# A decoder block's Out projection: its last block product made of seven inner products, interleaved with the sixth

## The chip, the cores and the metric

The kernel runs on one core of a Trainium2 chip. The metric is the device time of one launch in microseconds (us). A core has TensorE (PE, matrix products into PSUM), VectorE (DVE), ScalarE (ACT), GpSimd (POOL) and SyncE (SP); the last two issue most transfers here. Transfers move between the chip's memory (DRAM) and the on-chip SBUF, or inside SBUF.

## What is computed

One layer of a trunk on 512 tokens of width 2048: a windowed attention, its output projection, then a gate of embeddings and two norms. Cut to what matters:

```python
def swa_mixer(h, w_in, w_out, sinks, rel_bias):
    ...
    return (out * jax.nn.silu(gate)) @ w_out

def reference(x, p, norm_g, final_g, ...):
    hn = rmsnorm(x, norm_g[i])
    y = swa_mixer(hn, ...)
    x = x + y
    emb = p[i] @ ple_proj[i]
    g = jax.nn.sigmoid(rmsnorm(x, ple_norm[i]) @ ple_gate[i])
    x = x + emb * g
    return rmsnorm(x, final_g)
```

`w_out` and `ple_gate` are 2048 x 2048. The change touches the product with `w_out`.

## The kernel before

**Three matmuls for one.** Values are float32, but TensorE runs the faster type fp32r. So each operand is split in a high part (a cast on ScalarE) and a low part (the operand less its high part, on VectorE), and `mm3` (L120 to L126) issues three matmuls: high x high, high x low, low x high.

**Seven products for eight.** Out projection and gate projection cut both matrices in 2 x 2 blocks and make seven block products (numbers 1 to 7) in place of eight, from sums and differences of blocks. `ORDER_OUT` is 1, 7, 2, 6, 5, 3, 4. A block product multiplies 256 tokens by 1024 x 1024 weights. It runs over two column halves `jj`, four pieces of weights `m` in each (128 x 1024, 512 KiB, two chunks of 128 rows by 512 columns), two chunks `kk` and two token blocks `tb`: a piece is 12 matmuls, a block product 96. The last one, product 4, uses the activations' block 22 as it is.

**Weights.** `Pieces` (object `B`) numbers the pieces in the order of their use. `ahead(i)`, called as piece `i` is used, loads pieces up to `i + 3` on SP's queue and splits pieces up to `i + 2`: `bhi` on ScalarE (L641), `blo` on VectorE (L642). Raw, high and low parts have three buffers each (`wpool`). Sums of weight blocks for products 7, 5 and 6 are made in DRAM long before. Product 6's eight pieces are loaded into tiles `grown`; after their use, accumulating transfers on GpSimd's queue (L628) add block 21 of `w_out`, which makes product 4's pieces.

**Activations.** `Forms.steps(p)` makes the activations of product `p`: a subtraction in place (L734), then four times a cast `fh` and a low part `fl` (L746, L747), in eight buffers of `acts`.

**Results.** `add_y` adds each finished PSUM bank into `x1` on VectorE, once or twice (L955, L957), and where a block of `x1` is complete, `squares` sums its squares on ScalarE (L924). The functions waiting to be called stand in `later`; `some_later` issues them spread over the next pieces.

**Turns.** The gate projection needs `x1` transposed. `turn(kp, th, tag)` issues four transposes of 128 x 128 on TensorE into a PSUM bank (L938) and two copies scaled by `pn` on ScalarE (L941). Twelve of the sixteen turns stand in product 4, two after each of six pieces; the last four stand in the gate's first product.

**PSUM.** Four tags with two banks each: `s` and `p` hold product 1's two column halves, in whose banks 6, 5 and 3 go on, then product 4's; `t` and `o` hold those of products 7 and 2, then the turns of product 4.

**Order.** In this stage TensorE and SP run in the order written. VectorE, ScalarE and GpSimd get a fixed order from a planner when the program is built, so work whose buffers are free can stand well ahead of where it is written.

Of the kernel before, what the change touches and what calls it, by code (L numbers as in the profile page):

```python
# [11 lines left out]
F32 = mybir.dt.float32  # L12
# [8 lines left out]
P = 128  # L21
# [34 lines left out]
def trunk_kernel(ctx: ExitStack, tc: tile.TileContext, a: dict):  # L56
# [557 lines left out]
    class Pieces:  # L614
# [3 lines left out]
        def __init__(self):  # L618
            self.specs, self.base, self.made, self.grown, self.due = [], {}, {}, {}, []

# [16 lines left out]
        def _split(self, i):  # L637
            raw = self.base.pop(i)
            hi = wpool.tile([P, WE], F32R, tag="whi", name=f"bhi{i}")
            lo = wpool.tile([P, WE], F32R, tag="wlo", name=f"blo{i}")  # L640
            nc.scalar.copy(hi, raw)  # L641
            nc.vector.tensor_sub(lo, raw, hi.bitcast(F32))  # L642
            self.made[i] = tuple([t[:, :512], t[:, 512:]] for t in (hi, lo))

# [10 lines left out]
        def ahead(self, i):  # L655

            last = len(self.specs) - 9
            for n in range(max(i, 0), min(i + 6, last) + 1):
                kind = self.specs[n][0]
                if n not in self.base and n >= self.done and kind != "grow" and (kind == "seed" or n <= i + 3):  # L660
                    self._prepare(n)
            while self.done <= min(i + 2, last):
                self._split(self.done)
                self.done += 1

        def get(self, i):
            self.ahead(i)

            key = self.specs[i][2]
            if key is not None:  # L670
                n = next((n for n in range(i + 1, len(self.specs)) if self.specs[n][2] == key), None)
                if n is not None:
                    self.due.append((i + 6, n))
            while self.due and self.due[0][0] <= i:
                self._prepare(self.due.pop(0)[1])
            return self.made.pop(i)

    B = Pieces()

    def add_stage(nm, order):  # L680
        at = {}

# [5 lines left out]
        for p in order:  # L688
            for jj in range(2):
                if nm == "ple_gate" and (p, jj) == (4, 0):  # L690
                    for v in range(2):
                        at["e", v] = len(B.specs)
                        add_embeds(p, v)
                at[p, jj] = len(B.specs)
                for m in range(4):
                    if (nm, p) in SUMS:
                        src = summed[nm, p, jj, m]
                    else:
                        src = block(nm, *{1: (1, 1), 2: (2, 1), 3: (2, 2), 6: (1, 1), 4: (2, 1)}[p], jj, m)
                    growing = (6, 4) if (nm, 6) in SUMS else (7, 6, 4)  # L700
# [6 lines left out]
    at_out = add_stage("w_out", ORDER_OUT)  # L707
# [164 lines left out]
    rooms.append(late)  # L872
    x1 = [late.tile([P, NB, 512], F32, name=f"x1_{j}") for j in range(4)]
# [8 lines left out]
    def banks(p, jj, nm):  # L882
# [3 lines left out]
        tag = ("to" if p in (7, 2) else "sp")[jj]  # L886
# [40 lines left out]

    def turn(kp, th, tag):
# [10 lines left out]
        for n in range(2):  # L939
            k = 2 * kp + n  # L940
            nc.scalar.mul(hT[g][:, k % 4, th * 256 : th * 256 + 256], tp[:, n * 256 : n * 256 + 256], pn[:, k : k + 1])  # L941
# [20 lines left out]

    x_at = {(1, 1, 1): 0, (7, 0, 0): 2, (7, 0, 3): 1, (7, 1, 1): 3}
    waiting = {(7, 0): (1, 0), (2, 0): (1, 1)}
    held = {}
    for n, p in enumerate(ORDER_OUT):
        nxt = out_forms.steps(ORDER_OUT[n + 1]) if n < 6 else iter(())
        for jj in range(2):
            later.extend(held.pop(waiting.get((p, jj)), ()))
            calls = iter(range(4))  # L970

            def todo():
                part = x_at.get((p, jj, next(calls)))
                if part is not None:
                    load_x(part)
                next(nxt, None)
                if p == 4:
                    for tag in "to":
                        if turns:
                            turn(*turns.pop(0), tag)  # L980
                    if jj:
                        next(ple_first, None)

            ps = unit(p, jj, at_out, out_forms, todo)
            posts = [partial_of(add_y, p, jj, tb, ps[tb]) for tb in range(2)]
            if p == 1:
                held[p, jj] = posts
            else:
                later.extend(posts)
        run(nxt)  # L990
        if p == 6:
            nc.sync.dma_start(fg, a["final_g"].partition_broadcast(P))
        if p == 3:
            turns = [(kp, 0) for kp in range(8)] + [(kp, 1) for kp in range(4, 8)]
# [78 lines left out]
    spare = late.tile([P, 2 * WE], F32R, name="spare")  # L1073
    rooms4 = {}
    early = {(5, 0, 3): 0, (5, 1, 2): 1, (5, 1, 3): 2, (3, 0, 1): 3, (3, 0, 3): 4, (3, 1, 0): 5, (3, 1, 2): 6}
# [203 lines left out]
```

## Time and profile before

| | us |
|---|---|
| median of three runs | 799.04 (798.94 to 799.8) |
| the profiled execution | 798.73 |
| its span, first to last instruction | 797.0 |
| TensorE busy | 785.5 (99%) |
| VectorE busy | 590.5 (74%) |
| ScalarE busy | 482.7 (61%) |
| GpSimd busy | 149.6 (19%) |

The Out projection's matmuls run from 452.5 to 610.1 us of the span. A row of a group names the line, the engine, the operation and what it writes and reads (`out<-in`), with a count. In a timeline the first number is the start, the second the duration, both in us; the bracket at the end tells how long the engine was idle before and what ended that.

### The profile page before, as it was taken

To read this page: it belongs to the slowest core of one execution; us is meant where nothing else is said; L and a number is where in the kernel's file an instruction comes from. 1 tells how busy PE (TensorE), PEld (TensorE's weight loads), DVE (VectorE), ACT (ScalarE), POOL (GpSimd) and SP (SyncE) were. 2 spreads that over 40 slices of the span, in tenths; PEclk is the share of its full clock that TensorE was granted. 3 is DMA by queue.
4 is the path that set the end of the run, shared out by engine and by line. 5 is a ranking of instruction groups with operands and counts; after the bars stand their busy time and mean duration, and the time that the engine had idled before them with its cause. 6 is when DMAs were issued, how large, how long until landed. Compare 5 with 4: busy or idle time off the path is not lost.

```text
span 797.0 us, 11130 instructions
## 1 busy us (share of the span) xinstructions
PE 785.5 (99%) x3760; PEld 656.1 (82%) x3760; DVE 590.5 (74%) x1013; ACT 482.7 (61%) x992; POOL 149.6 (19%) x363
## 2 busy tenths in 40 slices
PE   9999999999999999999999999999999999999995
PEld 7888888888888888888888888888888888878884
DVE  4436478888877787787887898766656977979686
ACT  5632377677556766566665654555568756758545
POOL 0003013443243314332133200030000020200000
PEclk9999999999999999999999999999999999999998
DMA  8790586889687967879585578998503996885533
GB/s 336 279 212 11 187 237 180 235 211 260 175 226 193 220 199 211 213 207 260 155 220 135 151 267 312 353 258 249 197 26 118 358 208 211 163 212 194 176 106 106
DMA packets 44073, 163.99 MB, mean 206 GB/s; under 512 B 6304, under 2 KB 6944, under 8 KB 40176
## 3 DMA queue, kind: packets, MB, share of 16 engines
q1 hardware_dynamic: 36896, 129.01, 48.1%
q0 software_dynamic: 6832, 33.88, 23.0%
q8 instruction: 29, 0.48, 0.2%
q10 hardware_dynamic: 288, 0.39, 0.1%
q14 instruction: 28, 0.23, 0.1%
HBM read 157.44 MB, written 46.19 MB: 255 GB/s over the span
## 4 chain that ended last, share of the span: by engine, by line
PE 85%; issue 7%; DMA 3%; DVE 3%; POOL 1%; ACT 1%; SPq 0%; DVEq 0%; POOLq 0%; ACTq 0%
PE qps L126 7%; PE qps L124 7%; PE qps L125 7%; PE gps L124 7%; PE gps L125 7%; PE gps L126 7%; PE o L124 6%; PE o L126 6%; PE o L125 6%; PE s L401 2%; PE g L125 2%; PE g L126 2%; PE g L124 2%; PE o L523 2%; PE vps L228 2%
## 5 line engine op out<-in xcount | busy, mean ns | idle before, releaser
L642 DVE TENSOR_TENSOR blo<-braw,bhi 128x1024 fp32r<-128x1024 f32 x80 | 97.7, 1223 | 40.4 <-ACT bhi L641 40.2
L641 ACT CAST bhi<-braw 128x1024 fp32r<-128x1024 f32 x80 | 84.0, 1051 | 56.3 <-PE o L126 16.4
L124 PE MATMUL gps<-xh,whi 128*128 128x512 f32 x256 | 100.5, 393 | 0.0
L125 PE MATMUL gps<-xl,whi 128*128 128x512 f32 x256 | 100.0, 391 | 0.0
L126 PE MATMUL gps<-xh,wlo 128*128 128x512 f32 x256 | 99.9, 390 | 0.0
L503 POOL TENSOR_SCALAR_AFFINE_SELECT own<-r 64x256 fp32r<-64x256 f32 x96 | 61.2, 637 | 193.0 <-ACT r L484 109.3
L113 DVE TENSOR_TENSOR wlo<-wraw,whi 128x1024 fp32r<-128x1024 f32 x60 | 73.5, 1226 | 25.8 <-ACT whi L107 24.3
L124 PE MATMUL qps<-xh,whi 128*128 128x512 f32 x224 | 87.7, 392 | 0.0
L124 PE MATMUL o<-bhi,fho 128*128 128x512 f32 x224 | 87.7, 391 | 0.0
L125 PE MATMUL qps<-xl,whi 128*128 128x512 f32 x224 | 87.4, 390 | 0.0
L126 PE MATMUL qps<-xh,wlo 128*128 128x512 f32 x224 | 87.3, 390 | 0.0
L126 PE MATMUL o<-bhi,flo 128*128 128x512 f32 x224 | 87.2, 389 | 0.0
L125 PE MATMUL o<-blo,fho 128*128 128x512 f32 x224 | 87.2, 389 | 0.0
L461 ACT ACTIVATE t<-t,sm 128x129 f32<-128x129 f32 x128 | 50.6, 397 | 49.3 <-DVE sm L452 46.5
L125 PE MATMUL g<-blo,fhg 128*128 128x512 f32 x192 | 74.8, 390 | 0.4 <-DVE blo L642 0.4
L124 PE MATMUL g<-bhi,fhg 128*128 128x512 f32 x192 | 75.1, 391 | 0.0
L126 PE MATMUL g<-bhi,flg 128*128 128x512 f32 x192 | 74.8, 390 | 0.0
L107 ACT CAST whi<-wraw 128x1024 fp32r<-128x1024 f32 x60 | 62.1, 1037 | 16.1 <-DMA wraw<-in_w_q 16.1
L484 ACT CAST r<-pt 128x256 fp32r<-128x256 f32 x64 | 23.8, 372 | 55.4 <-PE pt L479 55.1
L126 PEld LDWEIGHTS gps<-xh,wlo 128*128 128x128 f32 x256 | 48.1, 188 | 10.6
L124 PEld LDWEIGHTS gps<-xh,whi 128*128 128x128 f32 x256 | 48.1, 188 | 9.1
L125 PEld LDWEIGHTS gps<-xl,whi 128*128 128x128 f32 x256 | 48.1, 188 | 8.7
(204 smaller groups left out, 1699.4 us busy)
## 6 DMA issues: line engine op xcount, KB each, us to landing
wraw<-in_w_gate_in SPq DMA_DIRECT2D x32, 512.0 KB, 5.4
wraw<-in_w_q SPq DMA_DIRECT2D x28, 512.0 KB, 6.2
w_out<-in_w_out POOLq DMA_DIRECT2D x24, 512.0 KB, 7.8
braw<-in_w_out SPq DMA_DIRECT2D x24, 512.0 KB, 4.0
braw<-in_ple_gate SPq DMA_DIRECT2D x24, 512.0 KB, 4.3
w_out<-in_w_out SPq DMA_DIRECT2D x16, 512.0 KB, 7.6
ple_gate<-in_ple_gate SPq DMA_DIRECT2D x16, 512.0 KB, 6.5
ple_gate<-in_ple_gate POOLq DMA_DIRECT2D x16, 512.0 KB, 6.1
```

Source lines behind the costliest of these rows:

```text
L107: nc.scalar.copy(hi, self.raw[i])
L113: nc.vector.tensor_sub(lo, raw, hi.bitcast(F32))
L124: nc.tensor.matmul(ps, sh, mh, start=first, stop=False, skip_group_check=more)
L125: nc.tensor.matmul(ps, sh, ml, start=False, stop=False, skip_group_check=more)
L126: nc.tensor.matmul(ps, sl, mh, start=False, stop=last, skip_group_check=more)
L228: nc.tensor.matmul(v_ps[t], h[:, c], both[:, :, 256:512], start=f, stop=e, skip_group_check=True)
L401: nc.tensor.matmul(s_ps[:, u, : 2 * n], st, key[:, :, first : first + n], start=True, stop=True)
L461: nc.scalar.activation(su, su, AF.Exp, bias=sm[:, u : u + 1], accum_out=sm[:, 2 + u : 3 + u])
L484: nc.scalar.copy(r[:, 0], PT[i])
L503: nc.gpsimd.affine_select(out=cols(own[places[g % 2 ^ low]]), in_=cols(r[here, low].bitcast(F32)), pattern=[[sign * QB, 2], [0, GROUP], [s ...
L641: nc.scalar.copy(hi, raw)
L642: nc.vector.tensor_sub(lo, raw, hi.bitcast(F32))
```

## The change

Product 4 (256 tokens by 1024 x 1024 weights) is cut once more in 2 x 2 blocks, and seven inner products of 128 tokens by 512 x 512 weights are made in place of eight. An inner product has two small steps `n` of 6 matmuls; there are 14. They are written between product 3's eight pieces (`SHARED`): eight of them, then six more at the end.

The weights of the inner products come from the eight grown tiles, four blocks of two tiles each. `Inside.sums` and `Inside.split` add them by transfers from SBUF to SBUF on GpSimd's queue: two copies of block 22 into `sum7`, and eight accumulating transfers. The links run: `sum7` = 22, `sum7` += 12, 12 += 11, and, when the first small product's pieces are split, 11 += `sum7`; after the fourth's, 21 += 11. The inner forms (`Inside.forms`) are made in place in activation block 22, seven of 128 x 512. Their order is 1, 7, 6, 2, 5, 4, 3.

From product 6 to near the end of this stage pieces are loaded four ahead and split three ahead, every fourth into the tile `spare` as a fourth buffer. The growing of a tile is written four pieces after its use and not six. The turns are spread: four in product 3, then one after each of several small steps and two together (kp 6 and 7) after the third of the last six. Those two are copied on VectorE. The load of `final_g` stands after the seventh small step. Product 2 of the gate takes the banks `s` and `p`.

Functions to be called later are now taken half at each step. The core of the diff:

```diff
         def _split(self, i):
-            raw = self.base.pop(i)
-            hi = wpool.tile([P, WE], F32R, tag="whi", name=f"bhi{i}")
-            lo = wpool.tile([P, WE], F32R, tag="wlo", name=f"blo{i}")
+            kind, whose, key = self.specs[i]
+            raw = whose.raw(*key) if kind == "part" else self.base.pop(i)
+            if self.first4 <= i < self.last4 and i % 4 == 3:
+                hi, lo = rooms[1][:, :WE], rooms[1][:, WE:]
+            else:
+                hi = wpool.tile([P, WE], F32R, tag="whi", name=f"bhi{i}")
+                lo = wpool.tile([P, WE], F32R, tag="wlo", name=f"blo{i}")
             nc.scalar.copy(hi, raw)
             nc.vector.tensor_sub(lo, raw, hi.bitcast(F32))
             self.made[i] = tuple([t[:, :512], t[:, 512:]] for t in (hi, lo))
+            if kind == "part":
+                whose.split(*key)
...
-                if n not in self.base and n >= self.done and kind != "grow" and (kind == "seed" or n <= i + 3):
+                if n not in self.base and n >= self.done and kind not in ("grow", "part") and (kind == "seed" or n <= i + (4 if self.first4 <= i < self.last4 - 2 else 3)):
                     self._prepare(n)
-            while self.done <= min(i + 2, last):
+            while self.done <= min(i + (3 if self.first4 <= i < self.last4 - 2 else 2), last):
                 self._split(self.done)
                 self.done += 1
...
-                    self.due.append((i + 6, n))
+                    self.due.append((i + 6, partial_of(self._prepare, n)))
+                elif key[0] == inside.nm:
+                    self.due.append((i + GROW, partial_of(inside.grow, key)))
...
+    GROW = 4
+    FOURTH = 24, 62
+    FINAL_G = 6
+    ORDER_IN = (1, 7, 6, 2, 5, 4, 3)
...
+        def grow(self, key):
+            nm, jj, m = key
+            nc.gpsimd.dma_start(B.grown[key], block(nm, 2, 1, jj, m), accum_op=ALU.add)
+        def begin(self):
+            s7 = rooms[0].tile([P, 2, 2, 512], F32, tag="partial", name="sum7", bufs=2)
+            self.s7 = s7.rearrange("p i k c -> p i (k c)")
+            self.t = {(kh, jj, i): B.grown[self.nm, jj, 2 * kh + i] for kh in range(2) for jj in range(2) for i in range(2)}
+        def sums(self):
+            for i in range(2):
+                nc.gpsimd.dma_start(self.s7[:, i], self.t[1, 1, i])
+                yield
+            for i in range(2):
+                self.grow_by(self.s7[:, i], self.t[0, 1, i])
+                yield
+            for i in range(2):
+                self.grow_by(self.t[0, 1, i], self.t[0, 0, i])
+                yield
+        def grow_by(self, out, more):
+            nc.gpsimd.dma_start(out, more, accum_op=ALU.add)
+        def raw(self, q, i):
+            if q == 7:
+                return self.s7[:, i]
+            return self.t[{1: (0, 0), 6: (0, 0), 5: (0, 1), 2: (1, 0), 4: (1, 0), 3: (1, 1)}[q] + (i,)]
+        def split(self, q, i):
+            if q == 1:
+                self.grow_by(self.t[0, 0, i], self.s7[:, i])
+            elif q == 2:
+                self.grow_by(self.t[1, 0, i], self.t[0, 0, i])
...
+        def forms(self):
+            v = lambda r, c: gates[2 + c][:, :, 256 + r * P : 256 + (r + 1) * P]
+            v11, v12, v21, v22 = v(0, 0), v(0, 1), v(1, 0), v(1, 1)
+            for q in ORDER_IN:
+                src, sub = {
+                    1: (v11, None), 7: (v11, (v21, v11)), 6: (v11, (v22, v11)), 2: (v12, None),
+                    5: (v21, (v21, v22)), 4: (v22, None), 3: (v12, (v12, v11)),
+                }[q]
+                if sub:
+                    nc.vector.tensor_sub(src, *sub)
...
+    SHARED = [(3, 0, 0), (3, 0, 1), "n", (3, 0, 2), "n", "n", (3, 0, 3), "n", (3, 1, 0), "n", "n", (3, 1, 1), "n", "n", (3, 1, 2), (3, 1, 3)]
+    SHARED += ["n"] * (14 - SHARED.count("n"))
+    OUT = [(p, jj, m) for p in (1, 7, 2, 6, 5) for jj in range(2) for m in range(4)] + SHARED
...
+    VECTOR_TURNS = {(6, 0), (7, 0)}
...
+            out, src = hT[g][:, k % 4, th * 256 : th * 256 + 256], tp[:, n * 256 : n * 256 + 256]
+            if (kp, th) in VECTOR_TURNS:
+                nc.vector.tensor_scalar_mul(out, src, pn[:, k : k + 1])
+            else:
+                nc.scalar.mul(out, src, pn[:, k : k + 1])
...
+    def inner_part():
+        x = None
+        for q in ORDER_IN:
+            if q in (1, 7, 2, 4):
+                ps = bank(f"o4_{q}", {1: "t", 4: "t"}.get(q, "o"))
+                x = ps if q == 1 else x
+            else:
+                ps = x
+            for i in range(2):
+                bh, bl = B.get(at)
+                fh, fl = inside.made[q]
+                for kk in range(2):
+                    k = 2 * i + kk
+                    mm3(ps, fh[:, k], fl[:, k], bh[kk], bl[kk], q in (1, 7, 2, 4) and k == 0, k == 3, q in (6, 5, 3))
+                if i == 1:
+                    coming.append(partial_of(add_in, q, ps))
+                yield
+    def add_in(q, ps):
+        whither = {
+            1: [((0, 0), -1)], 2: [((0, 0), 1)], 7: [((1, 1), 1), ((1, 0), -1)], 6: [((1, 0), -1)],
+            5: [((1, 1), 1)], 3: [((0, 1), 1)], 4: [((1, 0), 1)],
+        }[q]
+        for (r, c), sign in whither:
+            j, t = c, 2 + r
+            xt = x1[j][:, t, :]
+            if sign > 0:
+                nc.vector.tensor_add(xt, ps, xt)
+            else:
+                nc.vector.tensor_sub(xt, xt, ps)
+            if q in (2, 5, 3, 4):
+                squares(t, j)
...
+    extra = {
+        (5, 1, 0): [inside.begin, inner_sums, inner_sums], (5, 1, 1): [inner_forms, inner_sums, inner_sums],
+        (5, 1, 2): [inner_forms, inner_sums, inner_sums], (5, 1, 3): [inner_forms], (3, 0, 0): [inner_forms],
+        (3, 0, 1): [partial_of(turn, 0, 0, "o")],
+        (3, 0, 3): [partial_of(turn, 1, 0, "o")],
+        (3, 1, 0): [partial_of(turn, 2, 0, "o")],
+        (3, 1, 1): [inner_forms, partial_of(turn, 3, 0, "o")], (3, 1, 2): [inner_forms], (3, 1, 3): [inner_forms],
+        7: [partial_of(turn, 4, 0, "s")], 8: [partial_of(turn, 5, 0, "s"), ple_first],
+        9: [partial_of(turn, 4, 1, "o"), ple_first], 10: [partial_of(turn, 6, 0, "p"), partial_of(turn, 7, 0, "p")],
+        11: [partial_of(turn, 5, 1, "o"), ple_first],
+        12: [partial_of(turn, 6, 1, "o"), ple_first], 13: [partial_of(turn, 7, 1, "o")],
+    }
...
+    for at, step in enumerate(OUT):
+        if step == "n":
+            next(inner)
+            step, p = seen, None
+            seen += 1
+        else:
+            p, jj, m = step
+            if m == 0:
+                made[p, jj] = part(p, jj)
+                later.extend(held.pop(waiting.get((p, jj)), ()))
+            next(made[p, jj], None)
+        for _ in range(-(-len(later) // 2)):
+            later.pop(0)()
+        later.extend(coming)
+        coming.clear()
+        if step in x_at:
+            load_x(x_at[step])
+        if p in ahead:
+            next(ahead[p], None)
+            if (jj, m) == (1, 3):
+                run(ahead[p])
+        for f in extra.get(step, ()):
+            next(f, None) if hasattr(f, "send") else f()
+        if step == FINAL_G:
...
-                    turn(*turns.pop(0), "s")
+                    turn(*turns.pop(0), "t")
```

More of the change, by code (lines that the diff above doesn't have):

```diff
@@ L705, in add_stage @@
         return at
[L707 removed]
+    add_stage(inside.nm, ORDER_OUT)
     at_ple = add_stage("ple_gate", ORDER_PLE)
@@ L961, in trunk_kernel, with part @@
     turns = []
+    def part(p, jj):
+        ps = banks(p, jj, "o")
+        f = out_forms.made[p]
+        first = p not in (6, 5, 3)
+        for m in range(4):
+            fh, fl = f[m]
+            bh, bl = B.get(at)
+            for kk in range(2):
+                k = 2 * m + kk
+                for tb in range(2):
+                    mm3(ps[tb], fh[:, kk, blk(tb)], fl[:, kk, blk(tb)], bh[kk], bl[kk], first and k == 0, k == 7, not first)
+            if m == 3:
+                posts = [partial_of(add_y, p, jj, tb, ps[tb]) for tb in range(2)]
+                if p == 1:
+                    held[p, jj] = posts
+                else:
+                    coming.extend(posts)
+            yield
@@ L963, in trunk_kernel, with turns_of @@
+    def turns_of(*v):
+        for kp, th, tag in v:
+            turn(kp, th, tag)
     x_at = {(1, 1, 1): 0, (7, 0, 0): 2, (7, 0, 3): 1, (7, 1, 1): 3}
     waiting = {(7, 0): (1, 0), (2, 0): (1, 1)}
[L965 to L991, printed above, removed]
+    held, coming = {}, []
@@ new lines, in trunk_kernel @@
+    inner_sums, inner_forms = inside.sums(), inside.forms()
+    extra = {
[10 more added lines that the diff above has]
+    }
@@ L992, in trunk_kernel @@
             nc.sync.dma_start(fg, a["final_g"].partition_broadcast(P))
-        if p == 3:
-            turns = [(kp, 0) for kp in range(8)] + [(kp, 1) for kp in range(4, 8)]
+    turns = []
     run(ple_first)
```

52 lines of the change are left out of this document (44 added, 8 removed).

## The prediction

> **What bounds the kernel now.** I read the page's first two parts and its chain, then the waits of TensorE, then the stretches around the change.
>
> ```profile
> span 797.0 us, 11130 instructions
> PE 785.5 (99%) x3760; PEld 656.1 (82%) x3760; DVE 590.5 (74%) x1013; ACT 482.7 (61%) x992; POOL 149.6 (19%) x363
> ...
> PE 85%; issue 7%; DMA 3%; DVE 3%; POOL 1%; ACT 1%; SPq 0%; DVEq 0%; POOLq 0%; ACTq 0%
> ```
>
> ```profile
> PE warm_ps L145 <- PEq L1269: 0.8, 1, 0.8
> PE g L125 <- DVE blo L642: 0.4, 1, 0.4
> ```
>
> TensorE is busy for 99% of the span and is most of the chain. Its two longest waits are 0.8 and 0.4 us. So time is gained only by taking matmuls away, and lost only where TensorE starts to wait. The pace inside the Out projection, and the stretches it runs in:
>
> ```profile
> L126 PE MATMUL o<-bhi,flo x224: 389/389/397, 453.0 to 610.1; 128*128 128x512 f32 x112
> ...
> 540.06 0.39 PE L126 MATMUL o<-bhi,flo 128*128 128x512 f32 x1
> ...
> 542.78 0.39 PE L126 MATMUL o<-bhi,flo 128*128 128x512 f32 x1
> ```
>
> ```profile
> 539.70:561.40 21.70, 21.70 (x98) 17.96 (x97) 14.65 (x17) 11.68 (x17) 0.00 (x0) 1.00 0.77 246
> 561.40:583.20 21.80, 21.80 (x98) 18.06 (x97) 13.04 (x15) 11.36 (x17) 0.00 (x0) 1.00 0.50 169
> 583.20:610.30 27.10, 27.10 (x146) 22.93 (x145) 14.73 (x17) 22.03 (x45) 0.00 (x0) 1.00 0.06 20
> 625.00:650.00 25.00, 25.00 (x112) 20.70 (x111) 21.90 (x23) 15.18 (x21) 5.96 (x7) 1.00 1.04 277
> ```
>
> A matmul is shown with 0.39 us because matmuls overlap. What counts is from start to start: between the two rows lie 12 matmuls (one piece of weights: 2 halves x 2 token blocks x 3), 2.72 us, so 0.227 us each. A block product is 96 of them, 21.8 us. The rows of the stretches are length, then busy time of TensorE, weight loads, VectorE, ScalarE and GpSimd, granted clock, DMA share, GB/s. The first three are products 5, 3 and 4. VectorE is busy there for 68%, 60% and 54%, at a full clock (1.00). The fourth lies in the gate projection: VectorE 88%, DMA 104%, and by the waits above TensorE loses nothing there.
>
> **The saving.** Product 4 has 96 matmuls. Seven inner products of 4 weight chunks x 3 have 84, of the same shape (128x128 by 128x512). 12 x 0.227 = **2.72 us** less.
>
> **The transposes.** Twelve turns of four transposes stay, but they stood in six pairs and now stand alone, except one pair.
>
> ```profile
> 586.96 0.40 PE L125 MATMUL o<-blo,fho 128*128 128x512 f32 x1
> ...
> 590.60 0.40 PE L125 MATMUL o<-blo,fho 128*128 128x512 f32 x1
> ...
> 613.67 0.40 PE L125 MATMUL g<-blo,fhg 128*128 128x512 f32 x1
> ...
> 616.88 0.39 PE L125 MATMUL g<-blo,fhg 128*128 128x512 f32 x1
> ```
>
> The first two rows are one piece apart with a pair of turns: 3.64 - 2.72 = 0.92 us a pair (0.89 over the six pieces: 27.1 - 21.76 = 5.34 in all). The last two are one piece and a single turn apart: 3.21 - 2.72 = 0.49. Ten singles and a pair: 4.9 + 0.9 = 5.8 against 5.3, rounded sums of 5.74 and 5.36: **0.4 us** more.
>
> **Splits, forms and sums on VectorE and ScalarE.** Six more splits (14 small steps instead of 8 pieces), three more forms, four subtractions of forms, four more additions into x1. What one costs when another follows at once:
>
> ```profile
> 527.29 1.23 DVE L642 TENSOR_TENSOR blo<-grown,bhi 128x1024 fp32r<-128x1024 f32 x1 [1.45 <-ACT bhi L641]
> 528.44 1.28 DVE L957 TENSOR_TENSOR x<-x,o 128x512 f32<-128x512 f32 x2
> ...
> 539.61 1.28 DVE L957 TENSOR_TENSOR x<-x,o 128x512 f32<-128x512 f32 x2
> 540.80 0.68 DVE L747 TENSOR_TENSOR flo<-gate,fho 128x512 fp32r<-128x512 f32 x1
> 541.40 1.22 DVE L642 TENSOR_TENSOR blo<-braw,bhi 128x1024 fp32r<-128x1024 f32 x1
> ```
>
> ```profile
> 550.69 1.05 ACT L641 CAST bhi<-braw 128x1024 fp32r<-128x1024 f32 x1 [1.29 <-DVE blo L642]
> 551.65 0.62 ACT L924 ACTIVATE junk<-x 128x512 f32<-128x512 f32 x1
> 552.17 0.19 ACT L924 ACTIVATION_READ_ACCUMULATOR junk<-x 128x1 f32 x1
> 552.27 0.62 ACT L924 ACTIVATE junk<-x 128x512 f32<-128x512 f32 x1
> ...
> 553.18 0.62 ACT L746 CAST fho<-gate 128x512 fp32r<-128x512 f32 x1 [0.20 <-PE o L125]
> 553.71 1.05 ACT L641 CAST bhi<-braw 128x1024 fp32r<-128x1024 f32 x1
> ```
>
> ```profile
> 597.88 1.56 ACT L941 ACTIVATE hT<-tp,pn 128x256 f32<-128x256 f32 x4
> 599.31 0.65 ACT L924 ACTIVATE junk<-x 128x512 f32<-128x512 f32 x1
> ...
> L547 DVE TENSOR_TENSOR u<-o,tmp x64: 404/417/430, 118.6 to 456.0; 64x256 f32<-64x256 f32 x64
> ```
>
> From start to start, VectorE: a split 1.15, an addition or a form's low part 0.60. ScalarE: a split's cast 0.96, a square 0.62, a form's cast 0.53, half a turn's copy 1.43/4 = 0.36. Two turns' copies move to VectorE. No row has that operation; bounds are 0.36 (ScalarE's copy) and 0.68 (its 128x512 addition). The nearest row, a 256-wide read of PSUM on VectorE, has 0.42, which I take.
>
> Products 3 and 4 together are now 8 pieces and 14 small steps of 6 matmuls (1.36 us): 21.8 + 19.0 + 5.8 = 46.6 us. VectorE: 22 splits 25.3, 12 additions 7.2, 11 operations of inner forms 6.6, 4 low parts of the gate's first forms 2.4, four copies 1.7, together 43.2, or 93%. ScalarE: 22 x 0.96 + 11 x 0.53 + 8 x 0.62 + 20 x 0.36 = 39.1, 84%. On average both fit, and some inner forms go into product 5's 7 us of free VectorE time.
>
> The crowd is at the end. The last six small steps with seven turns last 6 x 1.36 + 5 x 0.49 + 0.9 = 11.5 us. In them fall, on VectorE, 5 splits 5.8, 4 low parts 2.4, 4 additions 2.4, 4 copies 1.7: 12.3. On ScalarE: 5 casts 4.8, 4 forms 2.1, 4 squares 2.5, 5 turns 3.6: 13.0. The excess is 0.8 and 1.5 us. Against it stands the lead of the splits. With a fourth buffer a split starts three steps ahead: 3 x 1.36 and two turns, 5.05, less cast and subtraction (1.05 + 1.22), is 2.8 us. So by starts nothing reaches TensorE: 0. By full durations (1.05, 0.62, 0.81 with its accumulator read, 0.47) ScalarE has 5.3 + 2.5 + 3.2 + 4.7 = 15.7, 4.2 too much, of which 2.8 is covered: 1.4 us. These are the bounds. The trace runs them back to back at the shorter spacing, so I take a value near the lower one: **0.3 us**. What would be late first is the pair of turns after the third of these steps. It reads x1 after product 3's last two additions, and they can start only when product 3 ends, as the first of these steps begins: 3 x 1.36 + 2 x 0.49 = 5.1 us for two additions of 0.6 with 0.4 of matmul tail, 3.5 us to spare. A late pair holds up every matmul behind it.
>
> **Transfers.** Removed from the way: nothing; the eight accumulating loads that made product 4's weights stay. Added: two copies and eight accumulating transfers from SBUF to SBUF on GpSimd's queue, in a chain: copy of block 22, + block 12, 12 += 11, then (after the first small product's split) 11 += sum. No row shows such a transfer. The nearest are the accumulating loads:
>
> ```profile
> L628 POOL DMA_DIRECT2D grown<-in_w_out x8: 847/856/885, 516.0 to 534.5; - x8
> L628 POOL DMA_DIRECT2D grown<-in_ple_gate x16: 847/855/873, 632.3 to 703.0; - x16
> DMA to landing us min/median/max: 5.1/7.6/11.7
> ...
> grown<-in_w_out POOLq DMA_DIRECT2D x8, 512.0 KB, 10.8
> ...
> fg<-in_final_g SPq DMA_DIRECT2D x1, 1024.0 KB, 16.3
> ```
>
> ```profile
> 520.00:540.00 20.00, 20.00 (x90) 16.57 (x89) 13.02 (x14) 9.98 (x14) 5.14 (x6) 1.00 1.06 239
> 545.02 1.05 ACT L641 CAST bhi<-braw 128x1024 fp32r<-128x1024 f32 x1 [3.86 <-DMA braw<-w_out]
> ```
>
> Issue to landing is 5.1 to 11.7 us; 10.8 is where the engines were full (1.06). The chain runs where the DMA share was 0.77, then 0.50. Ten transfers of 512 KiB at the 239 GB/s of the full stretch are 22 us of all engines. Free in the 540 to 592 us stretch are 5 + 11 + 8 = 24. I take the median, 7.6. The last block to be accumulated was issued at 534.5; the splits that free it now run one piece (2.7) sooner, so it lands at 534.5 - 2.7 + 10.8 = 542.6. Three links later, 565.4, the sums are ready. The last link also waits for the split of the first small product's second half, whose buffer comes free as product 3's first piece ends (561.4 + 2.72 + 2.3 = 566.4). It lands at 574.0. Its reader, the second half of the third small product, comes after five pieces, five small steps and three turns (561.4 + 13.6 + 6.8 + 1.5 = 583.3) and needs its split begun by 581.0. Spare: 7.0 us. Cost: **0**, as long as a link is under (581.0 - 542.6)/4 = 9.6 us.
>
> The ScalarE row is where cover is thinnest: product 5's fourth piece was waited for 3.86 us and was split at 545.02 + 1.05 + 1.22 = 547.3, 0.6 us before TensorE needed it (539.7 + 3 x 2.72 = 547.9). Now the first links fall there. But that load is asked for 2.7 us sooner, and the 1 MB load of final_g (16.3 us in flight, just ahead) moves behind. I cost it at nothing; uncovered, each us later than 2.7 + 0.6 is a us lost. Waiting links block only other links on GpSimd's queue: the next work of that queue, the gate's accumulating loads, starts at 632. SP's order gains one piece of lookahead; final_g and pT stay behind loads not needed for two pieces. Cost 0.
>
> **Sum.** -2.72 + 0.4 + 0.3 = -2.0. The profiled execution took 798.73 us (797.0 and 1.7 around it): 796.7, and a span of 795.0. The median of the three runs is 0.3 above it, so I predict **797.0**.
>
> **Rivals.** A, the links are late. If SBUF to SBUF keeps the 10.8 us of the full stretch, the chain ends at 542.6 + 43.2 = 585.8, 4.8 us after the split's latest start, and TensorE stands before the third small product. 4.8 - 2.3 is 2.5 slower: 801.5. It decides from 9.6 us a link, and turns the sign at 9.6 + 2.3/4 = 10.2. For it: ten more transfers in a chain, and the 11.7. Against: the engines are half free there, and the median is 7.6. Chance 0.13.
> The Trainium skill ("SBUF — State Buffer", section "SBUF: two separate sides") says that a DMA issued from GpSimd can be held up, since VectorE in some modes locks GpSimd out of the port that its descriptors are written through. The trace does not bear that out here: the 16 issues at 847 to 873 ns include those in the stretch with VectorE at 88%, as long as the eight beside an emptier VectorE. By the rule a link would grow by up to one 1.2 us subtraction, 7.6 to 8.8, which takes 1.2 of the 2.0 us that each has to spare and makes A nearer than the rows do.
>
> B, the crowd costs the gain. If VectorE has three splits and three low parts (3 x 1.15 + 3 x 0.6 = 5.3 us) ahead of product 3's last addition, the pair of turns waits 1.8 us beyond the 3.5 to spare: 799.0 - 2.3 + 1.8 = 798.5, no difference to be told. For it: 106% and 113% of work in that stretch. Against: the 88% stretch without a wait. Chance 0.20.
>
> C, a knot of banks. The third early turn takes the PSUM bank of the second small product, whose additions are written out a step later; the later turns alternate in two banks of which each waits for an evacuation. Where a split stands ahead of such an evacuation, TensorE waits for its cast and subtraction, 2.1 us. Three of those: 6.3 - 2.3, 803.0. Against: the pairs of turns before waited for no bank. Chance 0.07.
>
> That the change doesn't make fewer matmuls is excluded by the loops.
>
> **Chances.** About 0.2% (1.6 us) is what a measurement of this kernel can tell from no change. My forecast, 796.4 to 797.4 in its own range (no stall, or 1 us), has 0.60: faster. B 0.20: same. A and C 0.20: slower. The range 796.4 to 801.6 takes in A at 10.8 us a link and leaves out C and A's longer links, 0.12 together, and a little below.
>
> **What would show it.** Right: about 3748 matmuls; products 3 and 4 take 46.6 to 47.3 us; the links land in about 7 to 8 us; no wait of TensorE over 1 us stands between 561 and 612. Wrong: a wait of the third small product's split for a transfer (A), TensorE waiting at the turns for x1 (B), or links over 9.6 us.

## The result, and the profile after

| | before | after |
|---|---|---|
| median, us (lowest to highest) | 799.04 (798.94 to 799.8) | 796.54 (796.14 to 796.99) |
| ratio of the times | | 0.9965 [0.9954, 0.9977] |
| profiled execution, us | 798.73 | 796.17 |
| its span, us | 797.0 | 794.5 |

By the medians of seven executions each the change makes the kernel 2.5 us faster (0.31%), by the ratio 0.35%. The ratio is taken over all executions: their means, 799.26 and 796.48, give it. The page of the changed kernel, its head and its chain; a row of an engine has busy us, share of the span and number of instructions:

```profile
span 794.5 us, 11159 instructions
PE 782.9 (99%) x3748; PEld 653.8 (82%) x3748; DVE 604.7 (76%) x1034; ACT 489.0 (62%) x997; POOL 158.4 (20%) x373
...
PE 83%; issue 9%; DMA 2%; ACT 2%; POOL 2%; DVE 2%; DVEq 0%; POOLq 0%; SPq 0%; ACTq 0%
```

There are 12 matmuls fewer and 21 more operations on VectorE. TensorE is as full as before. Its longest waits:

```profile
PE warm_ps L145 <- PEq L1445: 0.9, 1, 0.9
PE g L125 <- DVE blo L647: 0.6, 1, 0.6
```

Neither stands in the Out projection: the second is the gate's old wait, 0.2 us longer. Where the 2.5 us come from is read from the first and last starts of two groups, the Out projection's first matmul and the gate's first matmul. Before:

```profile
L124 PE MATMUL o<-bhi,fho x224: 387/389/482, 452.5 to 609.6; 128*128 128x512 f32 x112
L124 PE MATMUL g<-bhi,fhg x192: 387/389/477, 610.3 to 756.4; 128*128 128x512 f32 x192
```

After, with the first matmul of product 3 from a timeline:

```profile
L124 PE MATMUL o<-bhi,fho x164: 389/389/476, 452.1 to 592.6; 128*128 128x512 f32 x164
L124 PE MATMUL g<-bhi,fhg x192: 388/389/476, 607.3 to 753.7; 128*128 128x512 f32 x192
...
560.94 0.39 PE L124 MATMUL o<-bhi,fho 128*128 128x512 f32 x1
```

At the trace's finer times the Out projection went from 157.76 to 155.23 us: 2.53 less, all of the gain of the span (2.5). (It starts 0.4 us sooner, and what follows it takes 0.4 longer.) Products 3 and 4 take 607.31 - 560.94 = 46.4 us. Of these 180 matmuls, at 2.72 us for 12, are 40.8, and 5.6 are left for the twelve turns, which took 5.34 before. The stretches around it (length, busy time of TensorE, weight loads, VectorE, ScalarE, GpSimd, granted clock, DMA share, GB/s):

```profile
539.70:561.40 21.70, 21.70 (x98) 17.96 (x97) 13.17 (x16) 10.43 (x15) 4.56 (x6) 1.00 1.03 306
561.40:608.00 46.60, 46.60 (x230) 38.69 (x229) 41.70 (x51) 38.33 (x68) 3.43 (x4) 1.00 0.65 176
596.40:608.00 11.60, 11.60 (x67) 9.74 (x66) 10.22 (x16) 11.59 (x25) 0.00 (x0) 1.00 0.09 13
```

VectorE is at 89% and ScalarE at 82% over the interleaved stretch, and in its last 11.6 us ScalarE is at 100%. TensorE still loses nothing there. The chain of transfers, in GpSimd's timeline (start, duration of the issue, and in brackets what GpSimd waited for), with the medians from issue to landing under it:

```profile
542.19 0.56 POOL L713 DMA_DIRECT2D sum<-grown  x1 [10.20 <-issue]
...
569.42 0.86 POOL L723 DMA_DIRECT2D grown<-sum  x1 [3.96 <-DVE blo L647]
...
sum<-grown POOLq DMA_DIRECT2D x4, 512.0 KB, 6.1
grown<-grown POOLq DMA_DIRECT2D x4, 512.0 KB, 8.1
grown<-sum POOLq DMA_DIRECT2D x2, 512.0 KB, 6.2
```

The first copy starts at 542.19 (forecast 542.6), the last link that product 4's third small product needs is issued at 569.42 and lands 6.0 us later, at 575.4 (forecast 574.0). So far the transfers are what was expected. How near they come to TensorE is seen from ScalarE and TensorE just after:

```profile
576.59 1.05 ACT L646 CAST bhi<-grown 128x1024 fp32r<-128x1024 f32 x1 [1.67 <-PE o L126]
577.55 0.83 ACT L1048 ACTIVATE hT<-tp,pn 128x256 f32<-128x256 f32 x2
...
580.96 0.60 PE L1041 MATMUL tp<-ident,x 128*128 128x128 f32 x4
```

The first row is the cast of the weights that the last link makes; it waited for a buffer that TensorE freed, 1.2 us longer than for the link. Behind it on ScalarE stand the two copies of the second turn. The third turn, at 580.96 on TensorE, goes into the PSUM bank that these copies empty. They end at 578.4, so there are 2.6 us to spare there and 1.2 between landing and cast: some 3.7 us in all.

### The profile page after: what moved, and what is told of

Its sections match the earlier page's. It is cut to its first block, busy times and chain, and to the rows that moved or that the text cites. A ratio compares the mean times of both kernels' runs of the same rounds, so it can differ in the third digit from the quotient of the medians.

```text
span 794.5 us, 11159 instructions
## 1 busy us (share of the span) xinstructions
PE 782.9 (99%) x3748; PEld 653.8 (82%) x3748; DVE 604.7 (76%) x1034; ACT 489.0 (62%) x997; POOL 158.4 (20%) x373
## 4 chain that ended last, share of the span: by engine, by line
PE 83%; issue 9%; DMA 2%; ACT 2%; POOL 2%; DVE 2%; DVEq 0%; POOLq 0%; SPq 0%; ACTq 0%
PE qps L124 7%; PE qps L126 7%; PE qps L125 7%; PE gps L124 7%; PE gps L125 7%; PE gps L126 7%; PE o L126 6%; PE o L124 6%; PE o L125 6%; PE s L401 2%; PE g L125 2%; PE g L126 2%; PE g L124 2%; PE vps L228 2%; PE o L523 2%
## 5 line engine op out<-in xcount | busy, mean ns | idle before, releaser
L647 DVE TENSOR_TENSOR blo<-braw,bhi 128x1024 fp32r<-128x1024 f32 x75 | 91.5, 1223 | 33.1 <-ACT bhi L646 32.8
L646 ACT CAST bhi<-braw 128x1024 fp32r<-128x1024 f32 x75 | 78.9, 1052 | 52.6 <-DMA braw<-in_w_out 11.5
L124 PE MATMUL o<-bhi,fho 128*128 128x512 f32 x164 | 63.9, 390 | 0.0
L126 PE MATMUL o<-bhi,flo 128*128 128x512 f32 x164 | 63.8, 389 | 0.0
L125 PE MATMUL o<-blo,fho 128*128 128x512 f32 x164 | 63.8, 389 | 0.0
```

What stands on the lines that cost most here:

```text
L124: nc.tensor.matmul(ps, sh, mh, start=first, stop=False, skip_group_check=more)
L125: nc.tensor.matmul(ps, sh, ml, start=False, stop=False, skip_group_check=more)
L126: nc.tensor.matmul(ps, sl, mh, start=False, stop=last, skip_group_check=more)
```

## The experiments

All run times below are medians of several runs; each ratio is against the kernel before on the same chip. Several kernels also differ by waits near 494 and 519 us, which come back at the end of this section.

**put_back.** The 12 matmuls are done again: in two of the inner products the first small step is multiplied twice with the same operands, and the accumulation starts over with the second time. Nothing else differs.

```diff
-                for kk in range(2):
+                twice = q in (7, 2) and i == 0
+                for n, kk in enumerate((0, 1, 0, 1) if twice else (0, 1)):
...
-                    mm3(ps, fh[:, k], fl[:, k], bh[kk], bl[kk], q in (1, 7, 2, 4) and k == 0, k == 3, q in (6, 5, 3))
+                    mm3(ps, fh[:, k], fl[:, k], bh[kk], bl[kk], q in (1, 7, 2, 4) and k == 0, k == 3 or (twice and n == 1), q in (6, 5, 3))
```

> The changed kernel with 12 matmuls put back: the first halves of the second and fourth inner products are multiplied twice, the first time into a group that the second one starts anew. Theory M (the time is TensorE's count: 12 x 0.227 = 2.72 us less, about 0.3 us more for turns, all else hidden): 796.5 + 2.7 = 799.2, 0.0% to 0.1% over the kernel before; the span from the Out projection's first matmul to the gate's is 2.7 us longer than in the changed kernel. Rival S (a part of the gain comes from the side edits, buffers, order of loads, later final_g): still faster than before by 0.5 us or more, under 798.5. Rival W (TensorE already waits in the changed kernel, the extra matmuls fill the wait): under 798.0.

Measured: 800.23 us, ratio 1.0007 [0.9997, 1.0016]. The whole gain is gone. In the profiled execution the Out projection takes 159.54 us, 4.3 more than in the changed kernel: 2.72 for the matmuls and 1.6, counted from start to start, around two places where TensorE waits for a low part (TensorE's timeline):

```profile
494.25 0.50 PE L125 MATMUL o<-blo,fho 128*128 128x512 f32 x1 [0.62 <-DVE blo L647]
...
519.39 0.50 PE L125 MATMUL o<-blo,fho 128*128 128x512 f32 x1 [0.30 <-DVE blo L647]
```

Both places are long before the edit.

**less_12.** The kernel before, without the 12 matmuls of the seventh piece of product 4; that part of the result is left out.

```diff
-            for kk in range(2):
+            for kk in range(0 if forms.nm == "o" and (p, jj, m) == (4, 1, 2) else 2):
```

> The kernel before without the 12 matmuls of product 4's seventh piece; its split stays, so one piece of product 4 is left out of the result. Theory M: 2.7 us less than before, 796.3, a ratio of 0.9966, about 0.3 us below the changed kernel since the turns stay in pairs. Rival S: the matmuls alone give less than the changed kernel has, so it stays above 797.0.

Measured: 797.16 us, 0.9966 [0.9954, 0.9977]; the Out projection takes 155.17 us, 2.59 less than before. Twelve matmuls less, with none of the change's other parts, give what the whole change gives. So the count sets the gain, and the parts around it cost TensorE about nothing in sum.

**scalar_turns.** No turn is copied on VectorE.

```diff
-    VECTOR_TURNS = {(6, 0), (7, 0)}
+    VECTOR_TURNS = set()
```

> The changed kernel with the two turns' four copies back on ScalarE: 4 x 0.36 = 1.4 us more there in the last six small steps, where ScalarE is busy for 11.6 of 11.6 us, 1.6 less on VectorE (10.2 of 11.6). Theory L: ScalarE runs late by up to 1.4 us, of which the lead of 1 to 2.8 us covers most: 796.5 to 797.9. Rival B of the prediction (no room left in that stretch): 1.4 us or more lost, over 797.9.

Measured: 796.44 us, 0.9962 [0.9949, 0.9975]; Out projection 155.19 us. Four copies more on ScalarE in its full stretch, four less on VectorE, and nothing moves: the crowd at the end costs nothing on either side of that choice.

**three_buffers.** Splits go back to three buffers and a lead of two steps, loads to a lead of three.

```diff
-    FOURTH = 24, 62
+    FOURTH = 0, 0
```

> The changed kernel without the fourth buffer: loads three ahead and splits two ahead as before. A small step of 1.36 us then leaves a split 2 x 1.36 (less 2.3 us of cast and subtraction) = 0.4 us of lead where two small steps stand together, and VectorE has 89% to do. Theory L (the lead is what hides the crowd): TensorE waits for blo at pairs of small steps and in the last six, 1 us or more at several of them, 2 to 6 us in all: 798.5 to 802.5. Rival (the splits have room anyway): within 0.5 us of the changed kernel, 796.5 to 797.0.

Measured: 798.16 us, 0.9983 [0.9973, 0.9993]; half of the gain is gone. TensorE's waits, one of them in its timeline, and the one weight load (PEld) that waits in the last six small steps:

```profile
PE o L125 <- DVE blo L647: 1.3, 2, 0.8
PE g L125 <- DVE blo L647: 1.1, 1, 1.1
...
563.41 0.50 PE L125 MATMUL o<-blo,fho 128*128 128x512 f32 x1 [0.76 <-DVE blo L647]
...
608.39 0.19 PEld L125 LDWEIGHTS o<-blo,ih 128*128 128x128 f32 x1 [0.38 <-DVE blo L647]
```

The Out projection takes 157.78 us, 2.55 more than in the changed kernel. Of the two waits of its matmuls the longer stands in product 3's first piece (third row), the other is the one near 494 us. Counted from start to start, the first loses 1.4 us, the one near 494 us 0.8, and the last row 0.35. The gate's wait is 0.5 us longer than in the changed kernel. The fourth buffer, with the longer leads that go with it, is worth some 1.4 us by the ratios (0.9983 - 0.9965 of 799), in low parts that are ready in time; the two intervals overlap a little.

**apart.** The fourteen small steps stand behind product 3 instead of among its pieces.

```diff
-    SHARED += ["n"] * (14 - SHARED.count("n"))
+    SHARED = [v for v in SHARED if v != "n"] + ["n"] * 14
```

> The changed kernel with all eight pieces of product 3 first and then the 14 small steps in a row. Theory L (interleaving is what keeps VectorE and ScalarE even): in the 14 steps and seven turns (14 x 1.36 + 3.4 = 22.4 us) VectorE has 14 splits 16.1, 8 additions 4.8, 4 low parts 2.4, copies 1.6, so 24.9; with a lead of 2.8 us at most 1 us is lost there; the link 21 += 11 has about 8 us from the fourth product's split to the sixth's, and links take 4.6 to 8.8: 0 to 2 us more. Out stage 156 to 158.5 against 155.2, time 797.5 to 800. Rival (order doesn't matter, since all work fits on average): within 0.3 us of the changed kernel's stage, 155.5 or less.

Measured: 800.72 us, 1.0011 [1.0000, 1.0022]. Here the additions into `x1` are late for the small steps that reuse their bank, and the gate's low parts too:

```profile
PE g L125 <- DVE blo L647: 1.6, 2, 1.3
PE o L124 <- DVE x L1120: 1.1, 1, 1.1
...
PE o L125 <- DVE blo L647: 0.5, 2, 0.3
PE o L124 <- DVE x L1118: 0.3, 1, 0.3
```

Without interleaving the small products lose at least what the 12 matmuls save, more than the expectation allowed (at most 800).

**longer_1 and longer_2.** The first link of the chain (the copies of block 22) is done twice, and three times: the same bytes again, so only the chain's length changes.

```diff
+            for _ in range(1):        # longer_2: range(2)
+                for i in range(2):
+                    nc.gpsimd.dma_start(self.s7[:, i], self.t[1, 1, i])
```

> The changed kernel with the first link of the chain done twice (both halves), about 5 us more in the chain of transfers, the values unchanged. In the changed kernel the last links landed at 571.0 and 575.4 and TensorE used the second half at 582.7, less 2.3 for the split: 5 us of room. Theory C (the chain is hidden with 5 us to spare): lost 0 to 0.7 us, out stage 155.2 to 155.9. Rival (the chain is bound by GpSimd's queue or the engines, or already waited for): 2 us or more lost.

> The same with the first link three times, about 10 us more. Theory C: the second half is about 5 us late, TensorE stands there: 4 to 6 us lost, out stage 159 to 161, slower than the kernel before: 800.5 to 802.5. Rival (links after the first overlap, or the planner moves other work into the gap): under 2 us lost.

Measured: longer_1 801.73 us (797.39 to 806.97 in ten runs), 1.0026 [0.9999, 1.0052]; longer_2 808.63, 1.0121 [1.0102, 1.0140]. In longer_1 the last link landed at 580.7, 5.3 us later than in the changed kernel and still ahead of the 581.0 that the prediction set as its limit. TensorE waited all the same (two waits, ScalarE's timeline, and the stretch behind the wait):

```profile
PE g L125 <- DVE blo L647: 1.6, 2, 1.2
PE tp L1044 <- ACT hT L1051: 1.4, 1, 1.4
...
580.80 1.05 ACT L646 CAST bhi<-grown 128x1024 fp32r<-128x1024 f32 x1 [2.28 <-DMA grown<-sum]
581.75 0.83 ACT L1051 ACTIVATE hT<-tp,pn 128x256 f32<-128x256 f32 x2
...
582.60:587.20 4.60, 4.56 (x22) 3.85 (x23) 4.14 (x7) 4.60 (x10) 0.00 (x0) 1.00 0.22 61
```

The second wait is not for the weights but for the turn's copies, which stand behind their cast: 5.3 late less 3.7 to spare is 1.6. In six of the ten executions of longer_1, from 801.6 us up, the granted clock over the span is 0.991 to 0.994, in the other four, the profiled one among them, 0.995 to 0.997. So TensorE also ran at a lower clock for some of the time in those six; where, was not traced. In longer_2 the same queue, with the last link 16 us late (591.4):

```profile
PE tp L1044 <- ACT hT L1051: 10.5, 1, 10.5
...
585.10 1.04 ACT L646 CAST bhi<-grown 128x1024 fp32r<-128x1024 f32 x1 [9.22 <-DMA grown<-sum]
591.54 1.04 ACT L646 CAST bhi<-grown 128x1024 fp32r<-128x1024 f32 x1 [5.39 <-DMA grown<-sum]
592.49 0.83 ACT L1051 ACTIVATE hT<-tp,pn 128x256 f32<-128x256 f32 x2
593.38 1.12 PE L1044 MATMUL tp<-ident,x 128*128 128x128 f32 x4 [10.52 <-ACT hT L1051]
...
593.40:598.00 4.60, 4.60 (x13) 3.83 (x14) 4.14 (x7) 4.60 (x10) 0.00 (x0) 0.51 0.17 46
```

ScalarE stands idle for 9.2 and 5.4 us with finished transposes behind the cast. TensorE itself ran 1.7 us late by earlier waits, most of them near 494 and 519 us, so what is left to wait is 16.0 less 3.7 less 1.7. After it the granted clock is 0.51 for 4.6 us, the last row, which adds some 2 us more. Both expectations were missed: 0 to 0.7 us were to be lost by longer_1 and 4 to 6 by longer_2, and it was 5 and 12 against the changed kernel.

**final_g_early and final_g_as_before.** The change moved the 1 MB load of `final_g` behind the loads of product 5, from 513.5 to 575.6 us. Here it is issued at the last piece of product 6, or at the one before, where it stood in the kernel before.

```diff
-    FINAL_G = 6
+    FINAL_G = 6, 1, 3        # final_g_as_before: 6, 1, 2
```

> The changed kernel with final_g's 1 MB loaded after product 6, as before. Theory D (its place is a cover for the loads of product 5): the accumulating loads and product 5's loads come 2.6 us later, the fourth piece's split, 3 us ahead in the changed kernel, keeps 0.4 us, the chain keeps 2.4: 0 to 0.5 us lost, out stage 155.2 to 155.7. Rival (the thin place breaks): 1 us or more lost at product 5's pieces.

> The changed kernel with final_g's load before the load that waits for the first of product 5's buffers, so that SP issues it at about 513 us as in the kernel before; in the earlier run it stood behind that load and went out at 536, in front of product 5's loads. Theory D2 (it was that place, 536, that cost 2.5 us of waits at 552 to 573; at 513 it only delays the grown tiles by 2.6 us, which have room): no waits over 0.3 us between 540 and 575, out stage 155.2 to 155.8 besides waits at 494 and 519. Rival (any place ahead of product 5 breaks the cover): 1.5 us or more lost between 540 and 575.

Measured: final_g_early 800.52 us, 1.0014 [1.0005, 1.0023]; final_g_as_before 799.29 (796.92 to 802.22), 0.9993 [0.9977, 1.0008]. The first takes the whole gain, the second nearly all of it, where 0 to 0.5 us and 0 to 0.6 were expected. In the profiled executions each does so in its own way. Early: SP's queue has it at 535.95, among the loads for product 5, and the splits behind are late (SP's timeline, then TensorE's):

```profile
535.95 0.60 SPq L1170 DMA_DIRECT2D fg<-in_final_g  x1
...
552.22 0.49 PE L124 MATMUL o<-bhi,fho 128*128 128x512 f32 x1 [0.27 <-ACT bhi L646]
553.48 0.50 PE L125 MATMUL o<-blo,fho 128*128 128x512 f32 x1 [0.77 <-DVE blo L647]
...
573.10 0.50 PE L125 MATMUL o<-spare,fho 128*128 128x512 f32 x1 [0.41 <-DVE spare L647]
```

As before: there is no wait of TensorE between 540 and 575 us. The loads that accumulate into product 4's weights are slower instead, and with them the chain, up to the same turn. The load and the accumulating loads of this kernel, the start of its chain, the wait, and TensorE behind it:

```profile
513.34 0.43 SPq L1170 DMA_DIRECT2D fg<-in_final_g  x1
...
grown<-in_w_out POOLq DMA_DIRECT2D x8, 512.0 KB, 14.5
...
546.60 0.56 POOL L713 DMA_DIRECT2D sum<-grown  x1 [14.41 <-issue]
...
PE tp L1041 <- ACT hT L1048: 2.1, 1, 2.1
...
585.51 0.63 PE L126 MATMUL o<-bhi,il 128*128 128x512 f32 x1
585.94 0.63 PE L124 MATMUL o<-bhi,ih 128*128 128x512 f32 x1
...
583.50:588.20 4.70, 4.70 (x16) 3.80 (x17) 4.24 (x7) 4.70 (x10) 0.00 (x0) 0.64 0.15 50
```

The same two rows of the changed kernel:

```profile
575.60 0.42 SPq L1170 DMA_DIRECT2D fg<-in_final_g  x1
...
grown<-in_w_out POOLq DMA_DIRECT2D x8, 512.0 KB, 10.4
```

From issue to landing the eight loads take 14.5 us in place of 10.4 (medians). So the chain starts 4.4 us later, its last link lands at 581.55, 6.1 later, and the third turn waits: 6.1 less 3.7 is 2.4 (its matmul starts 2.5 us after the one ahead, 2.3 more than usual). Eight matmuls then take 0.2 us more each, seven of them 0.427 us after the one ahead instead of 0.227: some 1.6 us. Together that is 3.9 of the 4.0 us by which this Out projection (159.19) is longer. It is the same chain and the same turn as in longer_1, made late by another transfer. The nine other executions have a granted clock of 0.996 to 0.997 over the span, and this one 0.994. So the fall of the clock is not shown for them; where they lose was not traced.

**after_again, x_sooner and x_sooner_pairs.** The changed kernel unaltered; with three of the four loads of `x` some pieces earlier, over products 1 and 7; and with ten turns in five pairs besides.

```diff
-    x_at = {(1, 1, 1): 0, (7, 0, 0): 2, (7, 0, 3): 1, (7, 1, 1): 3}
+    x_at = {(1, 0, 2): 0, (1, 1, 1): 2, (7, 0, 0): 1, (7, 1, 1): 3}
...
+        (3, 0, 1): [partial_of(turn, 0, 0, "o"), partial_of(turn, 1, 0, "o")],
...
+        8: [partial_of(turn, 4, 0, "s"), partial_of(turn, 5, 0, "s")],
+        9: [ple_first], 10: [partial_of(turn, 6, 0, "p"), partial_of(turn, 7, 0, "p"), ple_first],
+        11: [partial_of(turn, 4, 1, "o"), partial_of(turn, 5, 1, "o"), ple_first],
+        12: [ple_first], 13: [partial_of(turn, 6, 1, "o"), partial_of(turn, 7, 1, "o")],
```

> The changed kernel unaltered, beside a kernel before that on these chips ranges from 798.4 to 801.8. Theory V (the gain over the sum's 2.4 us lies in waits for loads at about 494 and 519 us of the span, early in the Out projection, that come in some executions of both kernels): ratio 0.9955 to 0.9980, times from 796.0 to 798.5 in steps, the Out stage 155.2 plus whatever waits stand at 494 and 519 in the profiled execution. Rival (the change itself gains 2.8 us or more): ratio under 0.9960 again and no wait there.

> The changed kernel with the first three 1 MB loads of x one to four pieces sooner, into the stretch from 457 to 477 us where the DMA share was 0.6, out of the 477 to 497 us one where it was 0.9. Theory V: the waits at 494 and 519 go, times gather near 796.2, and the median is 0.3 to 1.0 us under the changed kernel's beside it. Rival (these waits come from something else): same median and same spread as the changed kernel.

> The same with ten of the twelve turns in five pairs instead of one. Theory M: a pair costs 0.89 and two singles 0.95, four pairs more save 0.2 to 0.3 us of the Out stage, 155.0 against 155.2; nothing waits, since the gate's first forms have two steps to spare. Rival (a pair waits for its banks or makes the gate's first forms late): 0.3 us or more lost.

Measured, on one chip: after_again 796.95 us (796.11 to 798.37), 0.9966 [0.9953, 0.9979]; x_sooner 796.59 (796.32 to 796.96), 0.9960 [0.9947, 0.9973]; x_sooner_pairs 796.44 (795.99 to 796.50), 0.9957 [0.9944, 0.9970]. The last one in its two groups of matmuls:

```profile
L124 PE MATMUL o<-bhi,fho x164: 389/389/396, 452.2 to 592.2; 128*128 128x512 f32 x164
...
L124 PE MATMUL g<-bhi,fhg x192: 387/389/477, 607.2 to 753.5; 128*128 128x512 f32 x192
```

Its Out projection takes 155.03 us, 0.2 less than the changed kernel's: the pairs give back what the single turns cost. It beats the kernel before, and has the lowest ratio of all; against the changed kernel the difference lies inside the intervals, as x_sooner's does.

**The waits near 494 and 519 us.** They stand in the profiled executions of put_back, apart, longer_2 and final_g_early (three_buffers has the first), and not in those of the other seven, the kernel before or the changed one. Only x_sooner's edit touches that stretch, and three_buffers' its end from 517 us on. The runs of the unaltered changed kernel spread over 2.3 us on one chip, and those of x_sooner over 0.6, which would fit loads there that come late in some executions. With five and seven runs that isn't settled.

## Where the prediction was wrong, and where it was right

The mechanism was right: TensorE has 12 matmuls less to do and still doesn't wait in the Out projection. Two terms of the sum were too large: the turns were put at +0.4 us and cost 0.2, the crowd was put at +0.3 and cost 0. That makes the forecast gain 0.5 us too small, 797.0 against a median of 796.54. By the ratio the time is 799.04 x 0.9965 = 796.2, which is 0.2 us below the range's low end of 796.4; three of the seven executions lie below it too (796.14 twice, and 796.17).

**The saving** (-2.72) was right. It was priced by the distance of matmuls from start to start, not by their shown 0.39 us; put_back and less_12 show it from both sides.

**The turns** (+0.4) were too dear, and this step put the range wrong. The Out projection lost 2.53 us where the matmuls alone make 2.72, so turns and everything else cost 0.2. A single turn was priced at 0.49, from two rows of the gate. In the changed kernel 5.6 us for ten single turns and a pair of 0.89 leave 0.47 for a single one, and so do the same matmuls of two of the last small steps with a turn between them, 1.83 us apart where a small step is 1.36:

```profile
598.05 0.39 PE L125 MATMUL o<-blo,ih 128*128 128x512 f32 x1
599.88 0.40 PE L125 MATMUL o<-blo,ih 128*128 128x512 f32 x1
```

So each single turn was 0.02 us too dear, taken ten times. The range's low end, 796.4, is 798.73 - 2.72 + 0.4, the profiled time with no stall and with the turns at 0.4, so it had no room for a cheaper turn. Nor did it allow for what the medians of one kernel differ by (796.54 and 796.95 for the changed kernel).

**The crowd** (+0.3, between 0 and 1.4) cost 0, its lower bound. VectorE had 41.7 us of work in the stretch for 43.2 forecast, ScalarE 38.3 for 39.1. ScalarE's bound by full durations would have delayed TensorE by 1.4 us; ScalarE was full for the last 11.6 us and nothing was late. The lead of the fourth buffer is a part of what covers it: without it, three_buffers loses 0.35 us in the last six small steps, while its longer waits stand ahead of them. Rival B is false, by scalar_turns and by the missing wait at the pair of turns.

**The transfers** (cost 0) came out right by an argument that was partly wrong. Links took 4.6 to 8.8 us for 7.6 forecast, and the last one landed 1.4 late. But the spare was 3.7 us and not 7.0. The prediction set the limit by the reader on TensorE, the third small product at 583.3 us. The limit is set by what stands behind the reader's cast on ScalarE: the evacuation of a PSUM bank, for a turn at 580.96. That is rival C's knot reached through rival A's late link, and as two rivals with prices of their own neither was priced right: A was to cost nothing up to 9.6 us a link, and longer_1, whose last link landed within the prediction's limit of 581.0, ran 5 us over the changed kernel. Only the wait of 1.4 us, and a gate wait of 1.2, are seen in its profiled execution (799.19); where the executions of 801.6 us and more lost the rest was not traced.

The Trainium skill's rule that GpSimd's issues can be held up by VectorE ("SBUF — State Buffer", section "SBUF: two separate sides"), weighed in the prediction, isn't borne out by the links either: the four accumulating issues in the stretch with VectorE at 89% took 0.85 to 0.86 us, the four ahead of it, with VectorE at 61%, 0.85 to 0.88. The prediction counted a whole subtraction of 1.2 us for this rule, which is one for some modes of VectorE; no run here shows that these subtractions run in such a mode.

**The load of final_g** (cost 0) was to move out of the way of product 5's loads, where the prediction saw the cover at its thinnest, and nothing was put down for that. Moving the load is worth 2.2 and 3.9 us by the ratios of its two other places (0.9993 and 1.0014 against 0.9965); in the first of these it is the chain that comes late, and not product 5. So the move of this load isn't one of the small parts around the saving but a condition for it.

**Not priced at all** were what the interleaving and the fourth buffer each hold up: 3.7 us (apart, 1.0011 against 0.9965) and 1.4 us (three_buffers).

## What to carry to other kernels

Where one engine is busy for 99%, price a change by the matmuls it takes away, start to start, and then ask of each other part what would be late without it: here three of them (a fourth buffer, an interleaving, a moved load) are each worth half of the gain or more. A transfer's deadline is not its reader's: it is the first thing needed of whatever stands behind the reader's work in a fixed queue. A price that is the difference of two rounded measurements must keep its rounding in the range, at both ends.

## What the runs showed of the hardware

After a wait of TensorE the clock itself can fall. After 1.4 us (longer_1) the granted clock stayed at 1.00. After 2.1 us (final_g_as_before) it was 0.64 over the next 4.7 us, which is 3.4 us at half; eight matmuls took 0.2 us more each, 1.6 us in all. After 10.5 us (longer_2) it was 0.51 over the next 4.6 us, and the matmuls in it stood 0.427 us apart, which added some 2 us. The Trainium skill ("TensorE: Matmul & The Clock Gate", section "Part 1: The HAM clock gate") has the clock halved after about one idle window of 3.4 us. The stretch of half clock in final_g_as_before is as long as that window, but it came after a wait of 2.1 us; where between 1.4 and 2.1 us it begins, or whether it depends on when the wait falls, these runs don't tell.
